# Attention kernel on one Trainium2 core: a head's second group of sums stands in one piece, a copy and the last splits are tied behind other instructions

## The chip, the cores and the metric

The kernel runs on one core of a Trainium2 chip. The metric is the time of the whole kernel on the device, in microseconds, as the median of several runs. All engines named here belong to that core: the matrix engine (PE, with PEld for its weight loads), VectorE (DVE), ScalarE (ACT), GpSimd (POOL) and SyncE (SP), whose queue issues most of the loads and stores.

## The reference

One layer of a block of 1024 tokens and 1024 channels: attention without softmax (branch A), a short gated convolution (branch B), gates, an output projection, and a feed-forward part behind it. The change lies in the attention and in the first steps of branch A:

```python
# q, k, v: (B, S, H, Dh), S = 1024, H = 16 heads, Dh = 64
for i in range(s_len // Q_BLOCK):                 # Q_BLOCK = 128
    n_keys = i * Q_BLOCK + Q_BLOCK
    z = jnp.einsum('bhqd,bhkd->bhqk', qb, kp) * inv_sqrt
    mask = s_idx < t_idx
    log_not = jnp.where(mask, jax.nn.log_sigmoid(-z), 0.0)
    excl = lax.cumsum(log_not, axis=3, reverse=True) - log_not
    a = jnp.where(mask, jnp.exp(jax.nn.log_sigmoid(z) + excl), 0.0)
    outs.append(jnp.einsum('bhqk,bhkd->bhqd', a, vp))
...
merged = (jax.nn.sigmoid(ga) * (y_a @ w_branch_a[l])
          + jax.nn.sigmoid(gb) * (y_b @ w_branch_b[l]))
```

## The kernel before

Products that need nearly full float32 precision are made from two reduced parts of each operand, a high part (`...h`, a rounded copy made by ScalarE) and a low part (`...l`, what is left, made by VectorE). So most operands exist twice, and a "split" is a ScalarE copy followed by a VectorE subtraction.

**Steps.** Attention runs over 16 heads with 8 steps each. Step i of a head treats the queries of block i against (i + 1) blocks of 128 keys. A step has four parts.

- `att_scores` makes the scores on PE (lines L922 and L923) in tiles `z` of up to 512 columns. From step 4 on there are two such tiles: the narrow one first, then one of 512 columns. There are only two buffers for `z` in PSUM (`NZ` = 2), so a third tile has to wait until the sigmoid (ScalarE, L924) has read the first. GpSimd then masks the diagonal (L927).
- `att_scan` makes running products of the sigmoids with one scan on VectorE (L937). The scan's result is multiplied on GpSimd (through the helper `tt`, L133).
- `att_trans`, for the step two before, transposes the result on PE (L952) into one of three tiles `tr`. ScalarE (L957) and VectorE (L958) copy it out as high and low part, into `afh` and `afl` for whole groups and `ath` and `atl` for the triangular rest.
- `att_av` sums attention times values on PE (L969) into the one tile `o`. A head has two groups of four query blocks; the first group takes 8 matmuls, the second 16. When a group is complete, four ScalarE instructions (L975) move it out of PSUM to `oy`, VectorE adds to it (L977), and SP stores it to `d_ya` in DRAM (L978). The next group needs `o` again, so it cannot start before these are done.

A head's second group belongs to the step 7 of that head, so its sums are made while the next head's first steps run: in the kernel before a part of them in step 2 and the last part in step 3.

**Fillers.** Between these parts PE gets "fills": three matmuls each (L1034 to L1036) of the projection of branch B, which depend on nothing in the attention. How many go where follows from a running account. Each piece of attention yields a number (`F_Z`, `F_T`, `F_S`, and `F_A` by step), and fills are written out until their sum has caught up with the attention's. The order of PE, and that of the attention's instructions on VectorE and GpSimd, is the order in the code; a scheduler places the rest. `tc.issue_after(x)` ties an instruction behind another in that scheduling.

**Values.** For each head `att_dv` makes a high part `vt` of the values on ScalarE (L863) and a low part on VectorE (L133), in steps 4 and 6 of the head before.

**Branch A's inputs.** The stored sums come back as `yr` (a load by SP, L1187, of 256 KB into a ring of four buffers) and are split into `ya` (ScalarE L1189, VectorE L133). The loop over these 16 loads stands behind the attention in the code, but with high priority, so that the first splits stand between instructions of the last two heads:

```python
yr = fq.tile([P, 512], F32, tag=("ybh", "ybl")[j % 2], bufs=2, name=nm("yr"))
nc.sync.dma_start(yr, d_ya[n][:, k, :])
h_, l_ = ya2[:, 0], ya2[:, 1]
nc.scalar.activation(h_, yr, AF.Copy)
tt(nc.vector, l_, yr, h_.bitcast(F32), ALU.subtract)
```

The first 7 loads are of the first group of queries (heads 0 to 13), and the next of the second group. In branch A itself, VectorE multiplies PE's result by a gate (L1215).

Of the kernel before, what the change touches and what calls it, by code (L numbers as in the profile page):

```python
# [9 lines left out]
F32 = mybir.dt.float32  # L10
# [11 lines left out]
H = 16  # L22
# [8 lines left out]
def block_kernel(tc, x, x_t, cols, ada_1, ada_2, ada_row, w_q, w_kv, w_cg, w_a, w_b, w_o, w_g, w_u, w_d, out):  # L31
# [799 lines left out]

    F_Z, F_T, F_S, F_A = 0.2, 0.3, 0.05, (2, 0, 0, -1.3, 0, 0, 0, -0.7)

# [20 lines left out]
    def att_dv(h, part):  # L854

        va, vb = vab["va"], vab["vb"]
        cs = slice(h % 2 * DH, h % 2 * DH + DH)
        dv = vb[:, :, cs]
        if part == 0:
            tt(nc.vector, dv, dv, va[:, :, cs], ALU.subtract)  # L860
            return
        vt = vts[h] = bp.tile([P, KT, P], F32R, tag="vt", bufs=2, name=nm("vt"))
        nc.scalar.activation(vt[:, :, :DH], dv, AF.Copy)  # L863
        tt(nc.vector, vt[:, :, DH:], dv, vt[:, :, :DH].bitcast(F32), ALU.subtract)
# [35 lines left out]
    lastav = [None]  # L900
    lastz = [None]
    lastld = [None]
    npt = [0]
# [3 lines left out]
    def att_scores(h, i):  # L907
# [11 lines left out]
        for s0 in reversed(range(0, n, 512)):  # L919
# [3 lines left out]
            lastz[0] = nc.tensor.matmul(z[:, :m], sqt[:, i * P:(i + 1) * P], skl[:, s0:s0 + m], start=False, stop=True)  # L923
            nc.scalar.activation(pt[:, off + s0:off + s0 + m], z[:, :m], AF.Sigmoid, scale=rq[:, 1, i, h:h + 1])  # L924
            if s0 + m == n:
# [7 lines left out]
    def att_scan(h, i):  # L933
        pt, off = ptof[h, i], D - (i + 1) * P
        first = pt[:, slice(D - 1, off, -2)]
        both = pt[:, slice(D - 2, off - 1 if off else None, -2)]
        nc.vector.tensor_tensor_scan(out=both, data0=first, data1=both, initial=1.0, op0=ALU.mult, op1=ALU.mult)  # L937
        mid = pt[:, slice(off + 1, D - 2, 2)]
        tt(nc.gpsimd, mid, mid, pt[:, slice(off + 2, D - 1, 2)], ALU.mult)
# [45 lines left out]
    def attention():  # L985
# [3 lines left out]
        for s in range(len(steps) + DAV):  # L989
# [24 lines left out]
            if s < len(steps):  # L1014
                yield from (a_ for q in av[:1] for a_ in itertools.islice(q, (0, 0, 0, 1, 0, 0, 1, 0)[s % 8]))
            yield from tr_
            if s < len(steps):
                att_scan(*steps[s])
            for q in av[:1]:
                yield from itertools.islice(q, 9 if s >= len(steps) else (0, 0, 2, 2, 0, 0, 2 * (s > 8 * H - 8), 2)[s % 8])  # L1020

# [162 lines left out]
    with tc.high_priority():  # L1184
        for j, (ya2, (n, k)) in enumerate(zip(ya_slots(), [(0, k) for k in range(7)] + [(1, 0), (1, 1), (1, 2), (0, 7)] + [(1, k) for k in range(3, 8)])):
# [3 lines left out]
            nc.scalar.activation(h_, yr, AF.Copy)  # L1189
            tt(nc.vector, l_, yr, h_.bitcast(F32), ALU.subtract)  # L1190
            yah[n][k], yal[n][k] = h_, l_
# [618 lines left out]
```

## Time and profile before

| what | us |
|---|---|
| three runs | 1793.41, 1792.07, 1791.86 |
| their median | 1792.07 |
| the profiled execution | 1792.89 |
| its span in the trace | 1790.9 |

The rows further down come from the profiled execution. Its span is the time from the first to the last instruction that the profiler recorded; the 2.0 us between the span and the time of that execution lie around it. Attention lies between about 596 and 957 us of the span, the end of the last head's sums and branch A between 957 and 1012. Each engine takes its instructions in order, so an instruction that waits holds up all that is queued behind it on its engine. An idle gap in front of an instruction is put down to the event that came last.

### The profile page before, as it was taken

Reading aid. Unit: us, or ns where it says so; the run is one execution under the profiler, and the core shown is the slowest. Engines: PE = TensorE matmul, PEld = TensorE weight load, DVE = VectorE, ACT = ScalarE, POOL = GpSimd, SP = SyncE. Lnnn points to the kernel's source line nnn. Section 1 sums busy time; section 2 is a strip of 40 time slices with the busy share of each in tenths; the row PEclk is TensorE's granted clock in tenths of the full one; section 3 lists DMA queues with packets and bytes.
Section 4 is the critical chain, followed back from the end, with each engine's and each line's share of the span. In section 5 each row is a group of like instructions: output and inputs, shape, how many; then the busy total and the mean of one; then the engine's idle time right before and its main releaser. Section 6 shows DMA issues by size and latency. Waiting matters only on the chain.

```text
span 1790.9 us, 24256 instructions
## 1 busy us (share of the span) xinstructions
PE 1780.1 (99%) x8355; PEld 1471.0 (82%) x8355; DVE 1268.8 (71%) x1998; ACT 826.8 (46%) x1555; POOL 345.2 (19%) x437
## 2 busy tenths in 40 slices
PE   9999999999999999999999999999999999999999
PEld 6888877888888788888888888888888888888887
DVE  6876586778774677777786674698867777644766
ACT  5534364333433567666675221764544444432320
POOL 0024333733231243333341100100000000000000
PEclk9999999999999999999999999999999999999999
DMA  9579655222634967797654866324534344399776
GB/s 384 163 249 386 234 183 165 77 95 98 231 125 149 296 199 193 196 344 186 155 139 148 305 225 201 131 94 176 201 130 151 143 188 158 134 347 324 269 232 216
DMA packets 162446, 359.03 MB, mean 200 GB/s; under 512 B 15026, under 2 KB 56330, under 8 KB 161172
## 3 DMA queue, kind: packets, MB, share of 16 engines
q1 hardware_dynamic: 125740, 289.65, 48.7%
q10 hardware_dynamic: 33096, 55.25, 8.6%
q0 software_dynamic: 3488, 12.59, 1.9%
q8 instruction: 66, 1.08, 0.3%
q14 instruction: 56, 0.46, 0.1%
HBM read 247.84 MB, written 109.62 MB: 200 GB/s over the span
## 4 chain that ended last, share of the span: by engine, by line
PE 93%; DMA 3%; DVE 1%; ACT 1%; issue 1%; POOL 0%; SPq 0%; DVEq 0%; POOLq 0%; ACTq 0%
PE e L129 8%; PE e L128 8%; PE e L127 8%; PE pj L127 7%; PE pj L129 7%; PE pj L128 7%; PE pj L294 7%; PE pj L1034 4%; PE pj L1036 4%; PE pj L1035 4%; PE e L1637 4%; PE e L1638 4%; PE e L1639 4%; PE o L969 4%; PE tr L952 3%; PE z L922 2%
## 5 line engine op out<-in xcount | busy, mean ns | idle before, releaser
L1252 ACT ACTIVATE whi<-raw 128x512 fp32r<-128x512 f32 x137 | 85.2, 630 | 162.1 <-PE e L128 101.7
L1253 DVE TENSOR_TENSOR wlo<-raw,whi 128x512 fp32r<-128x512 f32 x137 | 93.4, 689 | 69.9 <-ACT whi L1252 52.5
L128 PE MATMUL e<-big,whi 128*128 128x512 f32 x352 | 136.9, 389 | 0.0
L127 PE MATMUL e<-big,whi 128*128 128x512 f32 x352 | 136.5, 390 | 0.0
L129 PE MATMUL e<-big,wlo 128*128 128x512 f32 x352 | 136.1, 389 | 0.0
L133 POOL TENSOR_TENSOR pt<-pt 128x63 f32<-128x63 f32 (+7 forms) x128 | 95.6, 747 | 209.8 <-DVE pt L937 166.2
L294 PE MATMUL pj<-whi,big 128*128 128x512 f32 x448 | 132.5, 393 | 1.3 <-ACT big L263 1.2
L133 DVE TENSOR_TENSOR c<-pj,c 128x512 f32<-128x512 f32 x140 | 93.7, 684 | 53.6 <-PE pj L129 52.9
L924 ACT ACTIVATE pt<-z,rq 128x128 f32<-128x128 f32 (+1 forms) x192 | 106.7, 581 | 52.6 <-PE z L923 43.9
L127 PE MATMUL pj<-big,whi 128*128 128x512 f32 x320 | 124.9, 390 | 0.0
L129 PE MATMUL pj<-big,wlo 128*128 128x512 f32 x320 | 124.7, 390 | 0.0
L128 PE MATMUL pj<-big,whi 128*128 128x512 f32 x320 | 124.6, 389 | 0.0
L1638 PE MATMUL e<-wlo,f 128*128 128x512 f32 (+1 forms) x319 | 121.8, 382 | 0.0
L1637 PE MATMUL e<-whi,f 128*128 128x512 f32 (+1 forms) x319 | 121.6, 382 | 0.0
L1639 PE MATMUL e<-whi,f 128*128 128x512 f32 (+1 forms) x319 | 121.6, 382 | 0.0
L1034 PE MATMUL pj<-big,whi 128*128 128x512 f32 x256 | 113.6, 444 | 0.0
L133 DVE TENSOR_TENSOR wlo<-raw,whi 128x512 fp32r<-128x512 f32 x108 | 86.6, 805 | 33.7 <-ACT whi L524 33.7
L524 ACT ACTIVATE whi<-raw 128x512 fp32r<-128x512 f32 x108 | 67.7, 631 | 89.1 <-PE pj L128 49.8
L127 PE MATMUL e<-rh,whi 128*128 128x512 f32 x264 | 102.7, 389 | 0.0
L128 PE MATMUL e<-rl,whi 128*128 128x512 f32 x264 | 102.7, 389 | 0.0
L129 PE MATMUL e<-rh,wlo 128*128 128x512 f32 x264 | 102.0, 389 | 0.0
L1036 PE MATMUL pj<-big,wlo 128*128 128x512 f32 x256 | 100.7, 393 | 0.0
(366 smaller groups left out, 4685.6 us busy)
## 6 DMA issues: line engine op xcount, KB each, us to landing
f<-d_f SPq DMA_DIRECT2D x77, 512.0 KB, 3.6
d_f<-fs SPq DMA_DIRECT2D x70, 512.0 KB, 2.8
raw<-w_cg SPq DMA_DIRECT2D x40, 512.0 KB, 3.9
raw<-w_u SPq DMA_DIRECT2D x26, 512.0 KB, 4.9
raw<-w_g SPq DMA_DIRECT2D x25, 512.0 KB, 3.5
raw<-w_kv SPq DMA_DIRECT2D x20, 512.0 KB, 6.4
ld<-ada SPq DMA_DIRECT2D x16, 512.0 KB, 9.0
d_t<-ts SPq DMA_DIRECT2D x16, 512.0 KB, 7.0
```

The costliest lines, as they stand in the source:

```text
L127: nc.tensor.matmul(ps, wh[:, k, :], fh[:, k, :], start=(k == 0 and not onto), stop=False, skip_group_check=onto)
L128: nc.tensor.matmul(ps, wh[:, k, :], fl[:, k, :], start=False, stop=False, skip_group_check=onto)
L129: last = nc.tensor.matmul(ps, wl[:, k, :], fh[:, k, :], start=False, stop=(k == 3), skip_group_check=onto)
L133: eng.tensor_tensor(out=out, in0=a, in1=b, op=op)
L294: nc.tensor.matmul(ps, a, b, start=(k == 0 and q == 0), stop=(k == KT - 1 and q == 2))
L924: nc.scalar.activation(pt[:, off + s0:off + s0 + m], z[:, :m], AF.Sigmoid, scale=rq[:, 1, i, h:h + 1])
L1034: nc.tensor.matmul(ps, wh, rh_, start=(k == 0), stop=False)
L1036: nc.tensor.matmul(ps, wl, rh_, start=False, stop=(k == KT - 1))
L1253: los.append(nc.vector.tensor_tensor(out=lo, in0=src, in1=hi.bitcast(F32), op=ALU.subtract))
L1637: nc.tensor.matmul(o, sh, w[0][:, c], start=(j == 0), stop=False)
L1638: nc.tensor.matmul(o, sh, w[1][:, c], start=False, stop=False)
L1639: nc.tensor.matmul(o, sl, w[0][:, c], start=False, stop=(j == NJ - 1))
```

## The change

Three edits. The number and kinds of instructions of every engine stay the same, and GpSimd's order too.

1. **The second group's sums.** All 16 matmuls of a head's second group now stand in step 2 of the next head. The numbers of pieces taken in a step change (`islice`), and with `F_A` the fill that stood before step 2's transposes goes behind those of step 3. The four evacuations of the sums on ScalarE move with them.
2. **The values' copy.** `vt`'s copy on ScalarE is tied behind the sigmoid that was written last, `lastsig`.
3. **Branch A's splits.** The VectorE half of the j-th split is tied behind one scan of the list `scans`: the first behind the last scan of head 14, the next ones behind one scan of head 15 each.

```diff
--- before.py
+++ after.py
@@ -829,7 +829,7 @@
     NPT = 5
     pts = [ptp.tile([P, D], F32, name=f"pt{j}") for j in range(NPT)]
 
-    F_Z, F_T, F_S, F_A = 0.2, 0.3, 0.05, (2, 0, 0, -1.3, 0, 0, 0, -0.7)
+    F_Z, F_T, F_S, F_A = 0.2, 0.3, 0.05, (1.6, 0, -0.6, -0.3, 0, 0, 0, -0.7)
 
     def att_load(h):
         pr, e0 = h // 2, (h % 2) * DH
@@ -860,7 +860,8 @@
             tt(nc.vector, dv, dv, va[:, :, cs], ALU.subtract)
             return
         vt = vts[h] = bp.tile([P, KT, P], F32R, tag="vt", bufs=2, name=nm("vt"))
-        nc.scalar.activation(vt[:, :, :DH], dv, AF.Copy)
+        with tc.issue_after(lastsig[0].ins):
+            nc.scalar.activation(vt[:, :, :DH], dv, AF.Copy)
         tt(nc.vector, vt[:, :, DH:], dv, vt[:, :, :DH].bitcast(F32), ALU.subtract)
 
     def load_vlast(e):
@@ -899,6 +900,8 @@
     first_va = v_tile(1)
     lastav = [None]
     lastz = [None]
+    lastsig = [None]
+    scans = []
     lastld = [None]
     npt = [0]
     ats = {}
@@ -921,7 +924,7 @@
             z = pps.tile([P, 512], F32, tag="z", bufs=NZ, name=nm("z"))
             nc.tensor.matmul(z[:, :m], sqt[:, i * P:(i + 1) * P], skh[:, s0:s0 + m], start=True, stop=False)
             lastz[0] = nc.tensor.matmul(z[:, :m], sqt[:, i * P:(i + 1) * P], skl[:, s0:s0 + m], start=False, stop=True)
-            nc.scalar.activation(pt[:, off + s0:off + s0 + m], z[:, :m], AF.Sigmoid, scale=rq[:, 1, i, h:h + 1])
+            lastsig[0] = nc.scalar.activation(pt[:, off + s0:off + s0 + m], z[:, :m], AF.Sigmoid, scale=rq[:, 1, i, h:h + 1])
             if s0 + m == n:
                 diag = pt[:, D - P:]
                 nc.gpsimd.affine_select(out=diag, in_=diag, compare_op=ALU.is_ge, fill=1.0, base=-1,
@@ -934,7 +937,7 @@
         pt, off = ptof[h, i], D - (i + 1) * P
         first = pt[:, slice(D - 1, off, -2)]
         both = pt[:, slice(D - 2, off - 1 if off else None, -2)]
-        nc.vector.tensor_tensor_scan(out=both, data0=first, data1=both, initial=1.0, op0=ALU.mult, op1=ALU.mult)
+        scans.append(nc.vector.tensor_tensor_scan(out=both, data0=first, data1=both, initial=1.0, op0=ALU.mult, op1=ALU.mult))
         mid = pt[:, slice(off + 1, D - 2, 2)]
         tt(nc.gpsimd, mid, mid, pt[:, slice(off + 2, D - 1, 2)], ALU.mult)
 
@@ -1012,12 +1015,12 @@
                 av[:] = [att_av(steps[s - DAV][0], steps[s - DAV][1] // 4)]
             yield from itertools.islice(tr_, 1)
             if s < len(steps):
-                yield from (a_ for q in av[:1] for a_ in itertools.islice(q, (0, 0, 0, 1, 0, 0, 1, 0)[s % 8]))
+                yield from (a_ for q in av[:1] for a_ in itertools.islice(q, (0, 0, 1, 0, 0, 0, 1, 0)[s % 8]))
             yield from tr_
             if s < len(steps):
                 att_scan(*steps[s])
             for q in av[:1]:
-                yield from itertools.islice(q, 9 if s >= len(steps) else (0, 0, 2, 2, 0, 0, 2 * (s > 8 * H - 8), 2)[s % 8])
+                yield from itertools.islice(q, 9 if s >= len(steps) else (0, 0, 3, 0, 0, 0, 2 * (s > 8 * H - 8), 2)[s % 8])
 
     def ps_f():
         return pps.tile([P, 512], F32, tag="pj", bufs=NPJ, name=nm("pj"))
@@ -1187,7 +1190,8 @@
             nc.sync.dma_start(yr, d_ya[n][:, k, :])
             h_, l_ = ya2[:, 0], ya2[:, 1]
             nc.scalar.activation(h_, yr, AF.Copy)
-            tt(nc.vector, l_, yr, h_.bitcast(F32), ALU.subtract)
+            with tc.issue_after(scans[min(len(scans) - 9 + j, len(scans) - 1)].ins):
+                tt(nc.vector, l_, yr, h_.bitcast(F32), ALU.subtract)
             yah[n][k], yal[n][k] = h_, l_
     fqpool.close()
     gxs = ExitStack()
```

**First place: head 8, steps 2 to 4, on PE.** `o` is the tile of head 7's second group, `z_7959` the narrow scores of step 4 and `z_7966` its wide ones; `tr_7936` is step 1's transposes, made in step 3. Before:

```order
L952 MATMUL tr_7936<-dm,pt_5131 128x128 x2
L969 MATMUL o_7920<-ath_7772,vt_7419 128x512
L969 MATMUL o_7920<-atl_7773,vt_7419 128x512
L969 MATMUL o_7920<-ath_7772,vt_7419 128x384
L969 MATMUL o_7920<-atl_7773,vt_7419 128x384
L969 MATMUL o_7920<-ath_7772,vt_7419 128x256
L969 MATMUL o_7920<-atl_7773,vt_7419 128x256
L969 MATMUL o_7920<-ath_7772,vt_7419 128x128
L969 MATMUL o_7920<-atl_7773,vt_7419 128x128
L922 MATMUL z_7959<-skh_7504,sqt_7503 128x128
L923 MATMUL z_7959<-skl_7505,sqt_7503 128x128
L922 MATMUL z_7966<-skh_7504,sqt_7503 128x512
```

With the change (`z_7941` are step 3's scores, line numbers 3 higher):

```order
L972 MATMUL o_7915<-ath_7772,vt_7419 128x128
L972 MATMUL o_7915<-atl_7773,vt_7419 128x128
L925 MATMUL z_7941<-skh_7504,sqt_7503 128x512
L926 MATMUL z_7941<-skl_7505,sqt_7503 128x512
L955 MATMUL tr_7948<-dm,pt_5131 128x128 x2
L1037 MATMUL pj_7896<-big_7562,whi_7574 128x512
L1038 MATMUL pj_7896<-big_7563,whi_7574 128x512
L1039 MATMUL pj_7896<-big_7562,wlo_7575 128x512
L925 MATMUL z_7959<-skh_7504,sqt_7503 128x128
L926 MATMUL z_7959<-skl_7505,sqt_7503 128x128
L925 MATMUL z_7966<-skh_7504,sqt_7503 128x512
L926 MATMUL z_7966<-skl_7505,sqt_7503 128x512
```

The last eight sums stood behind step 3's transposes and directly in front of step 4's scores. Now all sums are over before step 3's scores, and a fill (L1037 to L1039) stands between those transposes and step 4's scores.

The same place on ScalarE, before (`ath_7627` and `afh` are evacuations of transposes, `pt_5130` the sigmoid of step 3, `pt_5131` the two of step 4):

```order
L924 ACTIVATE pt_5129<-z_7617,rq 128x384
L957 ACTIVATE ath_7627<-tr_7629 128x128
L924 ACTIVATE pt_5130<-z_7644,rq 128x512
L957 ACTIVATE ath_7627<-tr_7651 128x2x128
L975 ACTIVATE oy_7666<-o_7635,vlast 64x128 x4
L924 ACTIVATE pt_5131<-z_7674,rq 128x128
L924 ACTIVATE pt_5131<-z_7681,rq 128x512
```

With the change:

```order
L927 ACTIVATE pt_5129<-z_7617,rq 128x384
L960 ACTIVATE ath_7624<-tr_7626 128x128
L978 ACTIVATE oy_7649<-o_7630,vlast 64x128 x4
L927 ACTIVATE pt_5130<-z_7656,rq 128x512
L960 ACTIVATE ath_7624<-tr_7663 128x2x128
L927 ACTIVATE pt_5131<-z_7674,rq 128x128
L927 ACTIVATE pt_5131<-z_7681,rq 128x512
```

The four evacuations of the sums (`oy`) have moved in front of step 3's sigmoid of 512 columns and an evacuation of transposes; they stood directly in front of step 4's two sigmoids.

**Second place: the end of head 14 and the start of head 15, on VectorE.** `pt_5131` and `pt_5127` are head 14's scans of steps 6 and 7 (the view names a scan SCALAR_TENSOR_TENSOR), `ya` the splits of branch A, `wlo` and `mb` work of branch B. Before:

```order
L133 TENSOR_TENSOR ya_9906<-yr_9907,ya_9906 128x512
L958 TENSOR_TENSOR atl_9449<-tr_9450,ath_9448 128x128
L937 SCALAR_TENSOR_TENSOR pt_5131<-pt_5131 128x448
L133 TENSOR_TENSOR ya_9921<-yr_9922,ya_9921 128x512
L133 TENSOR_TENSOR ya_9911<-yr_9912,ya_9911 128x512
L133 TENSOR_TENSOR ya_9916<-yr_9917,ya_9916 128x512
L958 TENSOR_TENSOR afl_9432<-tr_9467,afh_9431 128x4x128
L958 TENSOR_TENSOR atl_9449<-tr_9477,ath_9448 128x2x128
L937 SCALAR_TENSOR_TENSOR pt_5127<-pt_5127 128x512
L1086 TENSOR_TENSOR mb_9508<-pj_9376,sgi_9374 128x512
L977 TENSOR_TENSOR oy_9491<-o_9443,oy_9491 64x512
L133 TENSOR_TENSOR wlo_9800<-raw_9793,whi_9799 128x512
```

With the change:

```order
L940 SCALAR_TENSOR_TENSOR pt_5131<-pt_5131 128x448
L961 TENSOR_TENSOR afl_9432<-tr_9467,afh_9431 128x4x128
L961 TENSOR_TENSOR atl_9449<-tr_9477,ath_9448 128x2x128
L940 SCALAR_TENSOR_TENSOR pt_5127<-pt_5127 128x512
L133 TENSOR_TENSOR ya_9901<-yr_9902,ya_9901 128x512
L1089 TENSOR_TENSOR mb_9508<-pj_9376,sgi_9374 128x512
L980 TENSOR_TENSOR oy_9491<-o_9443,oy_9491 64x512
L133 TENSOR_TENSOR wlo_9800<-raw_9793,whi_9799 128x512
L961 TENSOR_TENSOR afl_9432<-tr_9527,afh_9431 128x4x128
L961 TENSOR_TENSOR atl_9449<-tr_9537,ath_9448 128x3x128
L940 SCALAR_TENSOR_TENSOR pt_5128<-pt_5128 128x64
L133 TENSOR_TENSOR ya_9906<-yr_9907,ya_9906 128x512
```

Four of these splits stood in front of the scan of head 14's step 7. Now none does; one stands behind that scan and one behind the first scan of head 15 (`pt_5128`).

On ScalarE the copies that belong to the later splits stand in head 15 now (`ya_9921` is the fifth, `ya_9926` the sixth; `pt_5129` to `pt_5131` are the sigmoids of steps 1 to 3). With the change:

```order
L960 ACTIVATE afh_9431<-tr_9527 128x4x128
L960 ACTIVATE ath_9448<-tr_9537 128x3x128
L927 ACTIVATE pt_5129<-z_9548,rq 128x256
L1192 ACTIVATE ya_9921<-yr_9922 128x512
L960 ACTIVATE afh_9431<-tr_9555 128x4x128
L960 ACTIVATE ath_9448<-tr_9565 128x4x128
L927 ACTIVATE pt_5130<-z_9577,rq 128x384
L960 ACTIVATE ath_9584<-tr_9586 128x128
L978 ACTIVATE oy_9609<-o_9590,vlast 64x128 x4
L1192 ACTIVATE ya_9926<-yr_9927 128x512
L927 ACTIVATE pt_5131<-z_9616,rq 128x512
```

Before, `ya_9921` stood in front of the evacuation `afh_9431<-tr_9467`, among the copies ahead of head 14's last transposes; `oy` stood behind `pt_5131`, and `ya_9926` between the two sigmoids of step 4. From `pt_5129` to `oy` there were evacuations and sigmoids only.

## Rows read from the trace of the kernel before

**Rows 1.** The page: busy time, share of the span and instructions of each engine.

```profile
PE 1780.1 (99%) x8355; PEld 1471.0 (82%) x8355; DVE 1268.8 (71%) x1998; ACT 826.8 (46%) x1555; POOL 345.2 (19%) x437
```

**Rows 2.** PE's weight loads' waits, 590 to 1015: waiter <- awaited: us, times, longest.

```profile
PEld z L922 <- ACT pt L924: 3.9, 16, 0.3
```

**Rows 3.** Timeline, PE, head 8: start, duration, line, tiles, count, [idle before, releaser].

```profile
783.86 0.38 PE L952 MATMUL tr<-dm,pt 128*128 128x128 f32 x2
784.00 0.47 PE L969 MATMUL o<-ath,vt 128*128 128x512 f32 x1
...
785.19 0.27 PE L969 MATMUL o<-atl,vt 128*128 128x128 f32 x1
785.30 0.28 PE L922 MATMUL z<-skh,sqt 128*128 128x128 f32 x1
...
785.53 0.44 PE L922 MATMUL z<-skh,sqt 128*128 128x512 f32 x1
785.81 0.40 PE L923 MATMUL z<-skl,sqt 128*128 128x512 f32 x1
786.05 0.49 PE L952 MATMUL tr<-dm,pt 128*128 128x128 f32 x3
786.29 0.49 PE L1034 MATMUL pj<-big,whi 128*128 128x512 f32 x1
...
787.08 0.28 PE L922 MATMUL z<-skh,sqt 128*128 128x256 f32 x1
787.20 0.28 PE L923 MATMUL z<-skl,sqt 128*128 128x256 f32 x1
787.51 0.50 PE L922 MATMUL z<-skh,sqt 128*128 128x512 f32 x1
787.85 0.39 PE L923 MATMUL z<-skl,sqt 128*128 128x512 f32 x1
```

**Rows 4.** Timeline of ScalarE, the same head.

```profile
784.12 0.69 ACT L924 ACTIVATE pt<-z,rq 128x512 f32<-128x512 f32 x1 [2.02 <-PE z L923]
...
785.50 1.13 ACT L975 ACTIVATE oy<-o,vlast 64x128 f32<-64x128 f32 x4 [0.41 <-PE o L969]
786.52 0.93 ACT L924 ACTIVATE pt<-z,rq 128x128 f32<-128x128 f32 x2
```

**Rows 5.** Timeline of PE, head 14, step 5.

```profile
926.55 0.45 PE L922 MATMUL z<-skh,sqt 128*128 128x512 f32 x1
```

**Rows 6.** Timeline of PE, the transposes of head 14's step 6.

```profile
937.24 0.28 PE L923 MATMUL z<-skl,sqt 128*128 128x256 f32 x1
938.67 0.66 PE L952 MATMUL tr<-dm,pt 128*128 128x128 f32 x4 [1.16 <-POOL pt L133]
```

**Rows 7.** Timeline of VectorE, ahead of head 14's last scan.

```profile
932.67 2.70 DVE L133 TENSOR_TENSOR ya<-yr,ya 128x512 fp32r<-128x512 f32 x3
...
936.22 1.21 DVE L937 TENSOR_TENSOR_SCAN pt<-pt 128x512 f32<-128x512 f32 x1
```

**Rows 8.** Timeline of ScalarE and of SP's queue, head 15 and behind.

```profile
937.61 0.47 ACT L924 ACTIVATE pt<-z,rq 128x256 f32<-128x256 f32 x1 [0.51 <-PE z L923]
...
959.67 1.27 SPq L1187 DMA_DIRECT2D yr<-d_ya  x3
...
962.63 0.63 ACT L1189 ACTIVATE atl<-yr 128x512 fp32r<-128x512 f32 x1 [1.58 <-DMA yr<-d_ya]
```

**Rows 9.** Groups by line: busy, mean ns of one, idle before and its releaser.

```profile
L958 DVE TENSOR_TENSOR afl<-tr,afh 128x512 fp32r<-128x512 f32 x64 | 44.0, 687 | 15.4 <-ACT afh L957 14.8
...
L957 ACT ACTIVATE afh<-tr 128x512 fp32r<-128x512 f32 x64 | 38.4, 600 | 17.7 <-PE tr L952 17.7
```

**Rows 10.** Timeline of PE, branch A's start.

```profile
1008.39 0.47 PE L1034 MATMUL pj<-ya,whi 128*128 128x512 f32 x1 [0.28 <-DVE sgi L1215]
```

**Rows 11.** Timeline of GpSimd: two multiplications of 447 columns, heads 7 and 14.

```profile
773.19 0.93 POOL L133 TENSOR_TENSOR pt<-pt 128x447 f32<-128x447 f32 x1 [1.79 <-DVE pt L937]
...
932.90 1.23 POOL L133 TENSOR_TENSOR pt<-pt 128x447 f32<-128x447 f32 x1 [2.40 <-ACT ya L1189]
```

## The prediction

> **What bounds the kernel now.** The page's busy line comes first: the matrix engine (PE) is busy for 99% of the span [rows 1], so nothing on the other engines counts unless it makes PE wait, and no work is added or taken away here. What can change is the sum of PE's waits in the attention stage (596 to 957 us) and in branch A behind it. The view of waits names them: PE's weight loads for scores waited 16 times for a sigmoid, 3.9 us in all [rows 2]. The timeline of one head shows where. In head 8 the scores of step 5 are ready to go at 787.32 (787.20 and a 128x256 matmul's 0.12, the distance of 787.08 and 787.20) and start at 787.51; the next start is 0.34 later instead of 0.23 [rows 3]. So a head loses 0.19 + 0.11 = 0.30 us there. The reason stands on ScalarE: the scores have two PSUM tiles (`NZ`), the third to come needs the sigmoid of step 4's second tile, and this one comes after four evacuations of sums, which begin at 785.50, 0.31 after the last matmul of the sums (785.19); ScalarE then goes to the next activation at 786.52 [rows 4]. Heads 1 to 13 have this wait. In head 14 a fill stands between the two scores of step 5 and there is none (no idle time in the row) [rows 5].
>
> **A head's second group summed in one piece.** PE keeps its instructions, but the eight last matmuls of the sums now come before step 3's scores, and a fill comes after step 3's transposes. On ScalarE the four evacuations move in front of step 3's sigmoid. Step 4's second scores need the PSUM tile that this sigmoid reads. I lay both engines out from the last matmul of the sums as zero, with head 8's durations.
>
> PE [rows 3]: 0.11 to step 3's scores (785.19 to 785.30); 0.28 for their first matmul behind a narrow one (785.53 to 785.81); 0.24 for the second (785.81 to 786.05); 0.14 for two transposes (783.86 to 784.00); 0.79 for the fill (786.29 to 787.08); 0.23 for step 4's two narrow scores (785.30 to 785.53). PE is ready for step 4's second scores at 1.79.
>
> ScalarE [rows 4]: evacuations begin at 0.31, step 3's sigmoid 1.02 later (785.50 to 786.52) and lasts 0.69 (the row at 784.12); PE goes on 0.06 after a sigmoid's end (786.52 + 0.93 = 787.45, against 787.51 [rows 3]). That is 2.08.
>
> So PE waits 0.29 at a new place; behind a wait the following start is 0.34 instead of 0.28 away (+0.06), and one more pair of wide scores stands behind a narrow matmul (0.28 for 0.23, +0.05). New cost 0.40, old cost 0.30: +0.10 a head. Step 5's wait should go, since step 4's sigmoid no longer queues behind the evacuations: it waits only for its own scores and is done about 0.3 us before PE asks. Heads 1 to 13: 13 x 0.10 = +1.3 us. Head 14 had no wait to give back: +0.40, of which some 0.05 were there, so +0.35. Bounds for a head: -0.30 (no new wait at all) and +0.40 (the old one stays too).
>
> **Values' copy behind the sigmoid.** One ScalarE instruction changes places with the first-needed sigmoid of step 5, a head's only move there. PE asks for that tile again at step 6's second scores, behind four transposes, a fill and the first scores; the old order did not make it wait there. Zero either way; if that cover went, one copy's 0.5 us a head would show.
>
> **Branch A's splits behind scans.** Before, three splits (2.70 us, each also waiting for its ScalarE half) stand ahead of head 14's last scan on VectorE [rows 7], and PE's transposes of that step start at 938.67, 1.31 after the 937.36 at which PE was free (937.24 and 0.12) [rows 6]. The tie puts the splits behind the scan. 2.70 is more than 1.31, so I take the whole 1.31 as won.
>
> What is late next is the ring of four loads `yr`. The fifth load needs the first split, which now stands behind this scan, and ScalarE's copy of the fifth stands in the order right behind the sigmoid of head 15's step 1 and in front of an evacuation that the sums need. The scan ended at 937.43 (936.22 + 1.21) [rows 7]; it moves up by at least 1.31 and at most 2.70, so its end is 934.7 to 936.1. Add a split, 0.69, and the load: issued 959.67, first reader at 962.63, so 2.96 [rows 8]. It is there at 938.4 to 939.8; ScalarE comes free at 938.08 (937.61 + 0.47) [rows 8], waits 0.3 to 1.7 and copies for 0.52 (a copy is 0.63 long and overlaps its neighbour by 0.1): the evacuation is 0.8 to 2.2 late. From the transposes' start PE has two sets of four transposes (some 0.34 each, since three take 0.24, 786.05 to 786.29 [rows 3]), two fills (0.79), one set of scores and a first sum (about 0.7) before the matmul that needs it: 3.0 us, against the 0.72 that ScalarE needs to come free there, then 0.60 and 0.69 of evacuation [rows 9], so some 0.95 is free. Loss 0 to 1.3; I take 0.8, nearer the late end, because the order in front of the scan keeps two evacuations. The sixth copy stands between head 15's four evacuations and its step 3 sigmoid: 0.40 + 0.52 = 0.9. Last head: -1.31 + 0.8 + 0.9 = +0.4; bounds -0.9 and +1.3 with a load of this length.
>
> The load's price can also be had from the Trainium skill, "DMA: Bandwidth & Descriptors", section "Anatomy of one DMA": about 2.0 us fixed and the bytes at 436 GB/s, which makes an estimated 2.6 us for 256 KB. By it the copy would wait 0.36 less and the last head come out near zero; the trace's 2.96 decides.
>
> **Branch A's own order.** The wait of PE at 1008.39, 0.28 for VectorE's product [rows 10], can go (the sums end earlier in PE's order, and what hangs on them too) or grow (VectorE has one more 1.2 us reduction in front of that product). I take -0.3, with bounds -0.5 and +0.5.
>
> Sum: +1.3 + 0.35 + 0.4 - 0.3 = +1.75, say +1.8. The profiled execution took 1792.89 us (its span 1790.9 and 2.0 around it), so it would be 1794.7; it stands 0.8 above the median of the runs shown. From the median 1792.07: **1793.9 us**, +0.1%. That is less than the 0.2%, 3.6 us, that a measurement of this kernel can tell from no change.
>
> **Rivals.**
> 1. *Faster: no new wait at step 4.* If step 3's sigmoid ends before PE is ready, 0.29 sooner than I have it, the 0.30 of 13 heads (3.9), the 1.31 and the 0.5 of branch A all go: -5.7, 1786.4. For it: it takes 0.29 only, and the first evacuation reads just the columns that are final earliest. Against it: in the trace that first evacuation starts only behind the last matmul [rows 3, 4], and the order of both queues is fixed. 0.13.
> 2. *Slower: ScalarE stands still behind late loads.* The copies wait in the middle of head 15, and each split frees the next load. If a load takes 3 us longer than the one in the row, it comes on top where no slack is left, first at the fifth copy and then, by half, at the sixth: +1.8 + 3 + 1.5 = +6.3, 1798.4. It decides from 0.5 us over the row on. For it: the ring has four buffers and the queue issues in order. Against it: few other transfers run there. 0.17.
> 3. *The tied splits meet the multiplication.* A scan's end releases GpSimd's multiplication, and the split now starts at that moment. The trace shows such a multiplication of 447 columns at 1.23 us beside splits and at 0.93 without [rows 11]. With 0.30 more on six multiplications in head 15, of which I let all gate PE, this gives +1.8 + 1.8 = +3.6, 1795.7; slack of about 1 us at most of them speaks against it. 0.12. The Trainium skill, "SBUF — State Buffer", section "Who interferes with whom", has such a rule: a VectorE instruction with two SBUF inputs and a GpSimd one that reads SBUF lock each other out for a whole instruction. By it the price would be a whole split each time; the trace shows less than half of one.
> 4. *The trade comes out even*, the new waits as long as those removed: 1791 to 1793. 0.18.
>
> **How the numbers follow.** My forecast (+1 to +3) has 0.40. Slower by over 0.2% comes from rival 2 and a part of rival 3: 0.20. Faster by over 0.2% is nearly all of rival 1: 0.13. The rest, 0.67, is within it. The range leaves out most of rival 1 and the upper part of rival 2: 1788.5 to 1797.0.
>
> **What will show it.** In the changed profile: scores of step 4 (not 5) with an idle gap near 0.3 and an activation as releaser, in heads 1 to 14; ScalarE's four evacuations directly before a 128x512 sigmoid; no wait of over 1 us at head 14's last transposes; a ScalarE wait for `yr` in head 15, with sums late behind it. I am wrong if the scores' waits vanish altogether, if step 5's wait stays beside the new one (+5), or if PE's waits of head 15 exceed 3 us.

## The result and the profile after

| | median us | runs |
|---|---|---|
| before | 1792.52 | 15 |
| changed | 1795.36 | 15 |

The ratio is 1.0016 (95% interval 1.0008 to 1.0023): +2.8 us, slower by less than the 0.2% taken as the bound. The changed kernel's profiled execution took 1797.45 us, the longest of its 15, so its span (1795.7) is not set against the old one; what is compared is PE's time head by head. The page's busy line and three of the waits of PE's weight loads (590 to 1020 us) answer to [rows 1, 2]:

```profile
PE 1781.3 (99%) x8355; PEld 1471.4 (82%) x8355; DVE 1269.3 (71%) x1998; ACT 825.0 (46%) x1555; POOL 341.9 (19%) x437
```

```profile
PEld z L925 <- ACT pt L927: 6.6, 16, 0.8
PEld tr L955 <- POOL pt L133: 5.9, 9, 1.6
PEld tr L955 <- DVE afl L961: 1.3, 3, 0.7
```

Busy times are the same within 0.1% on PE and DVE. Scores still wait 16 times for a sigmoid, but 6.6 us instead of 3.9. The place has moved, as PE's timeline of head 8 shows (answers to [rows 3]):

```profile
788.08 0.27 PE L972 MATMUL o<-atl,vt 128*128 128x128 f32 x1
788.19 0.44 PE L925 MATMUL z<-skh,sqt 128*128 128x512 f32 x1
...
788.84 0.47 PE L1037 MATMUL pj<-big,whi 128*128 128x512 f32 x1
...
789.67 0.27 PE L926 MATMUL z<-skl,sqt 128*128 128x128 f32 x1
790.14 0.50 PE L925 MATMUL z<-skh,sqt 128*128 128x512 f32 x1 [0.19 <-ACT pt L927]
790.47 0.39 PE L926 MATMUL z<-skl,sqt 128*128 128x512 f32 x1
```

And ScalarE's, same head (answers to [rows 4]):

```profile
788.39 1.12 ACT L978 ACTIVATE oy<-o,vlast 64x128 f32<-64x128 f32 x4 [2.35 <-PE o L972]
789.40 0.68 ACT L927 ACTIVATE pt<-z,rq 128x512 f32<-128x512 f32 x1
```

The last sums stand at 788.08, the evacuations begin 0.31 later, step 3's sigmoid starts 1.01 behind them and ends at 790.08, and PE goes on 0.06 after that. It was ready at 789.79 (789.67 and 0.12).

**PE's lost time by head.** For all that follows, the starts of neighbouring matmuls were taken from the trace, and from each distance the usual one for that width (0.23 us for 512 columns, 0.12 for 256); excesses over 0.045 us are summed from a head's first scores to the next head's. Some 0.42 us a head are left where nothing waits.

```
us lost by PE            0+1    2     3     6     8     12    14    15    branch A
before                   3.44  0.74  0.74  0.89  0.72  0.74  0.48  2.06  0.70
changed                  4.91  1.46  0.83  1.59  0.83  0.81  0.82  2.36  0.91
sums only                3.32  1.46  0.82  1.60  0.83  0.83  0.84  3.14  0.45
copy only                4.32  0.73  0.73  0.88  0.72  0.73  0.42  2.13  0.43
splits only              3.46  0.73  0.73  0.88  0.72  0.73  0.49  0.99  0.69
late evacuation          4.02  1.37  1.37  1.54  1.38  0.69  1.77  3.01  1.42
sums, add late           3.59  2.18  1.20  2.08  1.32  1.18  1.33  3.14  0.53
change, late evacuation  3.73  2.12  1.51  2.38  1.83  1.55  1.10  2.35  0.74
late evacuation, add     3.83  0.65  1.11  0.81  0.76  0.47  1.05  2.48  1.10
all three                3.18  0.67  1.14  0.85  0.79  0.42  0.48  1.32  2.05
splits and fill          3.36  0.42  0.42  0.59  0.42  0.42  0.42  0.92  0.49
behind transposes        3.72  0.42  0.47  0.58  0.42  0.42  0.42  0.59  0.48
change, fills shifted    3.43  0.83  0.83  0.99  1.57  0.94  0.84  2.27  1.36
change, behind transp.   2.56  1.15  0.42  1.11  1.01  0.42  0.85  1.45  0.79
```

Heads 3, 8 and 12 stand for those between; in the runs with late evacuations these differ among themselves. In heads 0 and 1 the engines also wait for transfers of branch B: ScalarE 1.6 us for weights before and 1.9 changed, VectorE 1.0 and 1.9 for the load of a `cy`. These heads differ by 0.9 us between the kernel before and the copy-only one, so the 1.5 us between two single executions there is put to no edit, though head 1 has the new wait at step 4 too. Branch A differs by up to 0.3 in the same way.

### The profile page after: what moved, and what is told of

The parts are those of the page before. It is cut to its first block, busy times and chain, and to the rows that moved or that the text cites. A ratio compares the mean times of both kernels' runs of the same rounds, so it can differ in the third digit from the quotient of the medians.

```text
span 1795.7 us, 24256 instructions
## 1 busy us (share of the span) xinstructions
PE 1781.3 (99%) x8355; PEld 1471.4 (82%) x8355; DVE 1269.3 (71%) x1998; ACT 825.0 (46%) x1555; POOL 341.9 (19%) x437
## 4 chain that ended last, share of the span: by engine, by line
PE 91%; DMA 3%; ACT 2%; DVE 2%; issue 1%; POOL 1%; SPq 0%; POOLq 0%; ACTq 0%; DVEq 0%
PE e L128 8%; PE e L129 8%; PE e L127 8%; PE pj L127 7%; PE pj L129 7%; PE pj L128 7%; PE pj L294 7%; PE e L1641 4%; PE e L1642 4%; PE e L1643 4%; PE pj L1037 4%; PE pj L1039 4%; PE pj L1038 4%; PE o L972 4%; PE tr L955 3%; PE e L1378 2%
## 5 line engine op out<-in xcount | busy, mean ns | idle before, releaser
L133 POOL TENSOR_TENSOR pt<-pt 128x63 f32<-128x63 f32 (+7 forms) x128 | 100.2, 783 | 200.5 <-DVE pt L940 165.5
L129 PE MATMUL pj<-big,wlo 128*128 128x512 f32 x320 | 124.7, 390 | 0.0
L1037 PE MATMUL pj<-big,whi 128*128 128x512 f32 x256 | 114.6, 448 | 0.0
L940 DVE TENSOR_TENSOR_SCAN pt<-pt 128x64 f32<-128x64 f32 (+7 forms) x128 | 96.1, 750 | 10.2 <-POOL pt L930 9.1
```

Source lines behind the costliest of these rows:

```text
L129: last = nc.tensor.matmul(ps, wl[:, k, :], fh[:, k, :], start=False, stop=(k == 3), skip_group_check=onto)
L133: eng.tensor_tensor(out=out, in0=a, in1=b, op=op)
L940: scans.append(nc.vector.tensor_tensor_scan(out=both, data0=first, data1=both, initial=1.0, op0=ALU.mult, op1=ALU.mult))
L1037: nc.tensor.matmul(ps, wh, rh_, start=(k == 0), stop=False)
```

## The experiments

Each is compared with the kernel before on the same chip.

**Sums only.** The change without its two ties:

```diff
-        with tc.issue_after(lastsig[0].ins):
-            nc.scalar.activation(vt[:, :, :DH], dv, AF.Copy)
+        nc.scalar.activation(vt[:, :, :DH], dv, AF.Copy)
...
-            with tc.issue_after(scans[min(len(scans) - 9 + j, len(scans) - 1)].ins):
-                tt(nc.vector, l_, yr, h_.bitcast(F32), ALU.subtract)
+            tt(nc.vector, l_, yr, h_.bitcast(F32), ALU.subtract)
```

> Only the sums are moved (the change's first edit); the values' copy and branch A's splits stand as before. Theory: the move alone carries the loss. In the heads without a delay on GpSimd the wait moves from step 5 to step 4 (idle gap 0.19 instead of 0.03 to 0.05, and +0.085 us a head, as in the trace of the changed kernel); in heads 1, 2 and 6, where a fill's VectorE work stands between the evacuation and step 3's scan, step 3's product comes late on GpSimd and costs some 0.5 more each; head 14's last transposes keep their 1.3 us. Sum: +1.1, +0.35 and +1.5, so 1.5 to 3.5 us slower than before. Rival (the splits carry the loss): within 1.5 us of before.

Measured: 1796.49 against 1792.95, ratio 1.0020 (1.0011 to 1.0029): +3.5 us. The steady heads lose 0.09 more each, heads 2 and 6 some 0.7 each, head 14 0.36; head 1 does not. Head 15, whose cost the expectation left out, loses 1.1: 0.9 of it in front of step 4's scores (950.35), where a copy `ya` stands between the four evacuations and step 3's sigmoid, as in the changed kernel. So this edit alone loses at least as much as the whole change.

**Copy only.** To the kernel before:

```diff
+        with tc.issue_after(lastsig[0].ins):
+            nc.scalar.activation(vt[:, :, :DH], dv, AF.Copy)
```

> Only the values' copy is tied behind the sigmoid of step 5. Theory: no cost and no gain, within 0.5 us of before by the starts of scores head by head (heads 3 to 13 each within 0.03 us of before). Rival (VectorE's low part of the values, which stands behind the copy, holds up the scan of step 5 or 6): 0.1 to 0.5 us a head, 1.5 to 7 us slower, with transposes that wait for GpSimd.

Measured: 1792.94 against 1792.95, 0.9998 (0.9989 to 1.0007). Heads 2 to 13 are within 0.03 of before each. The tie costs and brings nothing.

**Splits only.** To the kernel before:

```diff
+            with tc.issue_after(scans[min(len(scans) - 9 + j, len(scans) - 1)].ins):
+                tt(nc.vector, l_, yr, h_.bitcast(F32), ALU.subtract)
```

> Only branch A's splits are tied behind the scans. Theory: the 1.3 us of head 14's last transposes go; in head 15 ScalarE waits for the fifth load and some 0.8 us come back there; the sixth copy stands between step 4's two sigmoids, as before, so the 1.0 us wait of the changed kernel at step 4 isn't there. Net -0.3 us (-0.8 to +0.2) over heads 14 and 15, the other heads unchanged. Rival (the late loads cost more than the stall that they remove): +0.5 to +1.5 over heads 14 and 15.

Measured: 1790.92 against 1792.95, 0.9990 (0.9981 to 0.9999): faster by 2.0 us, of which the trace shows 1.07 in head 15. The 0.8 that I expected to come back did not, though ScalarE waits for the fifth load just as long (first fence; in the changed kernel 1.17). PE's timeline (second fence) has two fills (six matmuls) between the transposes whose evacuation stands behind that copy and the next ones, where the changed kernel has one:

```profile
939.76 0.64 ACT L1191 ACTIVATE ya<-yr 128x512 fp32r<-128x512 f32 x1 [1.20 <-DMA d_mb<-mb]
```

```profile
937.83 0.60 PE L954 MATMUL tr<-dm,pt 128*128 128x128 f32 x4
938.18 0.48 PE L1036 MATMUL pj<-big,whi 128*128 128x512 f32 x1
...
938.96 0.40 PE L1036 MATMUL pj<-big,whi 128*128 128x512 f32 x1
...
939.65 0.60 PE L954 MATMUL tr<-dm,pt 128*128 128x128 f32 x4
```

**Late evacuation.** To the kernel before; the four evacuations go behind step 4's sigmoids:

```diff
+        if g:
+            yield 0
         yv = bp.tile([DH, 512], F32, tag="oy", bufs=2, name=nm("oy"))
...
+            with tc.issue_after(lastsig[0].ins) if g and h < H - 1 else ExitStack():
-... islice(q, (0, 0, 0, 1, 0, 0, 1, 0)[s % 8])
+... islice(q, (0, 0, 0, 1, 1, 0, 1, 0)[s % 8])
-... islice(q, ... (0, 0, 2, 2, 0, 0, 2 * (s > 8 * H - 8), 2)[s % 8])
+... islice(q, ... (0, 0, 2, 1, 0, 0, 2 * (s > 8 * H - 8), 2)[s % 8])
```

> The kernel before, but the four evacuations of a head's second group are tied behind step 4's two sigmoids (heads 0 to 14); PE's order stays. Theory: step 5's wait is there only because step 4's sigmoids queue behind the evacuations, so it goes: -0.30 us a head in heads 1 to 13, -3.9 us (-3 to -4.5), and nothing new. Rival (ScalarE is short anyway and the wait comes up at step 6, or the transposes' evacuations come late for the next sums): between -1 and +2 us, with a new gap at step 6 or in front of the first group's sums.

Measured: 1801.41 against 1792.95, 1.0045 (1.0033 to 1.0058). Both theories missed: the scores' wait went but for 1.3 us in all, and transposes now wait for GpSimd's product, 0.73 in head 7, less in heads 9 to 13. Head 7, ScalarE, VectorE and PE:

```profile
768.58 1.11 ACT L979 ACTIVATE oy<-o,vlast 64x128 f32<-64x128 f32 x4
769.58 0.48 ACT L958 ACTIVATE ath<-tr 128x384 fp32r<-128x384 f32 x1
```

```profile
770.09 0.56 DVE L959 TENSOR_TENSOR atl<-tr,ath 128x384 fp32r<-128x384 f32 x1 [1.68 <-ACT ath L958]
770.68 0.69 DVE L981 TENSOR_TENSOR oy<-o,oy 64x512 f32<-64x512 f32 x1
771.30 0.81 DVE L938 TENSOR_TENSOR_SCAN pt<-pt 128x320 f32<-128x320 f32 x1
```

```profile
773.03 0.66 PE L953 MATMUL tr<-dm,pt 128*128 128x128 f32 x4 [0.73 <-POOL pt L133]
```

Two things hold up step 4's scan: the low part `atl`, which waits for the evacuation `ath` behind the four others, and the addition.

**Sums, with the addition late.** To the sums-only kernel, with step 3 taking one piece more:

```diff
+        if g:
+            yield 0
         nc.vector.tensor_tensor(out=yv, in0=o[DH:], in1=yv, op=ALU.add)
```

> As the run with the sums alone moved, but VectorE's addition of the evacuated sums (and its store) stands behind step 3's scan instead of in front of it. Theory: in heads 2 and 6 the scan came late because that addition waited for the evacuations at the head of VectorE's queue, with a fill's product behind it; so the 0.69 us of each of these heads go (each then 0.05 to 0.15), the 0.19 us gap at step 4's second scores stays in all heads: 1.2 to 1.6 us faster than the sums-only run, 1.7 to 2.3 us slower than before. Rival (the late sigmoid of step 3 alone makes the scan late, or the fill's product): heads 2 and 6 keep at least 0.5 us each.

Measured: 1800.97 against 1793.43, 1.0041 (1.0029 to 1.0054). The theory fell: heads 2 and 6 got worse (2.18 and 2.08), others too. Behind the scan the addition pushes the values' subtraction `vb` into GpSimd's product, where it takes 1.10 instead of 0.67, and the next scans come later.

**The change with late evacuation.** Sums in step 2, evacuations (tie as above) and addition in step 3, behind its scan:

```diff
+            with tc.issue_after(lastsig[0].ins) if g and h < H - 1 else ExitStack():
-... (0, 0, 3, 0, 0, 0, 2 * (s > 8 * H - 8), 2)[s % 8])
+... (0, 0, 3, 1, 0, 0, 2 * (s > 8 * H - 8), 2)[s % 8])
```

> The changed kernel, but the four evacuations of a second group (heads 0 to 14) are tied behind step 3's sigmoid, and VectorE's addition stands behind step 3's scan. Theory: step 4's wait was the queueing of that sigmoid behind the evacuations, so no scores wait in heads 3 to 13: 0.46 us a head less than the changed kernel at that place, and step 5's wait does not come back, since step 4's sigmoids have the fill in front of their scores. 5 to 7.5 us faster than the changed kernel, 2.5 to 4.5 faster than before. Rival (ScalarE is short, the wait comes up elsewhere): the gap moves to step 5, as in the kernel before, and the gain over the changed kernel is 1 to 2.5 us.

Measured: 1805.19 against 1793.43, 1.0065 (1.0053 to 1.0078). Both missed: most of the waits of PE's weight loads are now transposes that wait for GpSimd (18.8 us in all, 590 to 1025 us), and scores still wait for a sigmoid 26 times, 7.1 us.

**Late evacuation with the addition behind the scan.** As the late evacuation, with the last piece taken after step 4's scan:

```diff
-... (0, 0, 2, 2, 0, 0, 2 * (s > 8 * H - 8), 2)[s % 8])
+... (0, 0, 2, 1, 1, 0, 2 * (s > 8 * H - 8), 2)[s % 8])
```

> The kernel before with the evacuations tied behind step 4's sigmoids, as in the run that lost 8 us, but with VectorE's addition behind step 4's scan. Theory: that run lost because the addition stood in front of the scan and waited there for the late evacuations, so that GpSimd's product and the transposes came late by 0.73 us a head; the addition's place alone turns it round: no wait for GpSimd in heads 3 to 13, no wait for a sigmoid either, 3 to 4.5 us faster than before. Rival (the late evacuations hold up the transposes' evacuations on ScalarE): still 2 us or more slower than before, with the same gap at the transposes.

Measured: 1794.98 against 1793.43, 1.0007 (0.9998 to 1.0017), between the two ranges. The addition's place explains much of the 8 us but not all; head 3 still loses 1.11.

**All three.** The same, with the copy and the splits tied as in the change.

> The kernel before, with the copy tied behind the sigmoid and the splits tied behind scans as in the change, and with the evacuations behind step 4's sigmoids and the addition behind step 4's scan; the sums stay in steps 2 and 3. Theory: the gains add, 3.9 us of the scores' waits and 1.2 us of the splits: 4.5 to 6 us faster than before. Rival (the sixth copy, which now stands ahead of step 4's sigmoids in head 15, waits for its load there): 1 us of it is lost in head 15, with a scores' gap of about 0.7 us at its step 4 or 5.

Measured: 1793.08 against 1793.43, 0.9995 (0.9986 to 1.0005). Both missed. The splits' gain is there (head 15: 1.32); the scores' gain is not in heads 3 to 8. Branch A lost 1.4 more in this execution, in waits for ScalarE's weight copies (0.71 at 960.32) and for VectorE's product with the gate (0.47 and 0.44 at 1008.88 and 1014.89).

**Splits and fill.** The splits-only kernel, with one fill moved between step 5's two scores:

```diff
             if s0:
-                yield F_Z
+                yield F_Z + (0.8 if i == 5 and h else 0)
-        yield F_Z + F_S * ((i - 1) % 8 + 1) + (F_A[i] if h else 0)
+        yield F_Z + F_S * ((i - 1) % 8 + 1) + (F_A[i] if h else 0) - (0.8 if i == 5 and h else 0)
```

> The kernel before with the splits tied behind the scans (as in the splits-only run), and with the fill that stands just behind step 5's scores (behind its transposes in heads 1 and 2) put between the narrow and the wide scores, as heads 14 and 15 have it already; ScalarE's order stays. Theory: step 5's wait goes because 0.7 us of other work now covers it, and nothing hangs on that fill. PE's lost time a head falls from 0.74 to 0.42 us in heads 1 to 13, which is 4.0 us, and the splits give 1.2: 4.5 to 6 us faster than before. Rival (step 5's later wide scores hand the wait on to its scan, to GpSimd and to the transposes of step 7, as in the runs with late evacuations): at least 0.25 us a head comes back there, 1 to 2.5 us faster than before.

Measured: 1788.10 against 1792.89, 0.9977 (0.9969 to 0.9986): 4.8 us faster than before, as the theory had it, while the changed kernel was 2.8 slower. Nothing waits in step 5 of head 8:

```profile
786.25 0.28 PE L925 MATMUL z<-skl,sqt 128*128 128x256 f32 x1
786.37 0.40 PE L1036 MATMUL pj<-big,whi 128*128 128x512 f32 x1
...
787.06 0.39 PE L924 MATMUL z<-skh,sqt 128*128 128x512 f32 x1
787.28 0.39 PE L925 MATMUL z<-skl,sqt 128*128 128x512 f32 x1
```

**Evacuation behind the transposes' own.** All three, with another tie:

```diff
-            with tc.issue_after(lastsig[0].ins) if g and h < H - 1 else ExitStack():
+            with tc.issue_after(lastth[0].ins) if g and h < H - 1 else ExitStack():
```

(`lastth` is ScalarE's last evacuation of transposes, L961 there.)

> As the run with all three, but the late evacuations are tied behind ScalarE's evacuation of step 4's transposes, so this one comes before them. Theory: the runs with late evacuations lost their gain because that evacuation of transposes stood behind four others, VectorE's low part waited for it at the head of its queue, and the scan of step 4 behind it came late; so the small waits for GpSimd at step 6 go too, and PE's lost time falls to 0.42 us in heads 3 to 13: 0.23 less in heads 4 to 8, 0.7 and 0.45 less in heads 3 and 11. 1.5 to 4 us faster than the run with all three. Rival (ScalarE has no place for four evacuations in steps 4 and 5 at all): heads 3 to 8 keep 0.65 us or more and step 5's scan is late in the place of step 4's.

Measured: 1788.28 against 1792.89, 0.9973 (0.9963 to 0.9983). Heads 2 to 14 stand at 0.42 to 0.47 but for head 6 (0.58), and the gain over the run with all three is above the 4 us expected, since branch A and head 15 are lower here as well. So the place of `ath` was the other half of what the late evacuations had lost.

**The change with its fills shifted.**

```diff
-    HEAD, TAIL = 16, 10.0
+    HEAD, TAIL = 15, 10.0
```

> The changed kernel with one fill fewer ahead of the attention (15 for 16), which shifts the fills against the heads. In the changed kernel VectorE's product and split of a finished branch B block stand around step 3's scan in heads 2 and 6 alone, and these two lose 1.46 and 1.59 us of PE's time where other heads lose 0.83. Here neither head has that product ahead of step 3's scan nor the split behind it. Theory: the extra 0.65 to 0.75 us belongs to these VectorE instructions, so heads 2 and 6 fall to 0.75 to 1.1 us. Rival (it belongs to what else happens in heads 2 and 6, such as their loads): both stay above 1.3 us. The heads from 7 on get another pattern of fills and are not compared.

Measured: 1797.43 against 1792.89, 1.0026 (1.0016 to 1.0037). Heads 2 and 6 lose 0.83 and 0.99: the extra belonged to the fills' VectorE work. The whole is slower because of the heads from 7 on (head 8: 1.57).

**The change with evacuations behind the transposes' own.** The same tie and piece on the changed kernel:

```diff
-... (0, 0, 3, 0, 0, 0, 2 * (s > 8 * H - 8), 2)[s % 8])
+... (0, 0, 3, 0, 1, 0, 2 * (s > 8 * H - 8), 2)[s % 8])
```

> The changed kernel (second group's sums all in step 2, copy and splits tied) with the evacuations of heads 0 to 14 tied behind ScalarE's evacuation of step 4's transposes and VectorE's addition behind step 4's scan, as in the run before this one. Theory: the place of the sums on PE costs nothing by itself; the change lost through where the evacuations and the addition came to stand. So heads 2 to 14 fall to 0.42 us each (from 0.83, and from 1.46 and 1.59 in heads 2 and 6); in head 15 the wait behind the fifth copy stays (0.4 to 0.8 us more there than in the run that has the sums in two pieces). 5.5 to 7.5 us faster than the changed kernel, 3 to 5 faster than before. Rival (one piece of 16 sums costs by itself): heads 3 to 13 keep at least 0.6 us each, at most 4 us faster than the changed kernel.

Measured: 1791.33 against 1793.11, 0.9991 (0.9982 to 1.0000), short of the 3 us expected. Heads 3 and 12 fall to 0.42, so 16 sums in one piece cost nothing there. Heads 2 and 6 keep 1.1: a fill's product `cy` still stands directly ahead of step 3's scan in them, which the sums' place decides through the fills. In head 2 it starts at 648.12, the scan at 648.72, and the transposes that wait for GpSimd at 650.51 lose 0.66; in head 6 they lose 0.46. The extra of head 8 (1.01) is spread over several places, the largest of them 0.24 in front of step 4's wide scores.

## Why the prediction was right, point by point

The forecast was 1793.9, from a sum of +1.8; measured is +2.8, in the range and on the side forecast. One term failed, that of heads 2 and 6; the fifth load's came out near its number partly by luck; branch A's is within what two executions differ by.

- *The new wait at step 4.* Forecast 0.29 and a new cost of 0.40 a head, for 0.30 given back. The trace has 0.35 (790.14 less 789.79) and lost times of 0.83 and 0.74 over the 0.42 that is always there: 0.41 new, 0.32 old. Step 5's wait went. Head 14: +0.35 forecast, +0.34 measured.
- *Heads 2 and 6: the step that failed.* I wrote "heads 1 to 13: 13 x 0.10", so one head stood for all, and I followed the sums only along PE and ScalarE to the scores. On VectorE the addition moved too: before, it stood behind step 3's scan, now it stands ahead of it. And with the sums the fills moved: in heads 2 and 6 a fill's product (`cy`) now stands between the addition and that scan, and its split (`ybl`) behind. Head 2 before, then with the change on VectorE, GpSimd and PE:

```profile
648.40 0.68 DVE L937 TENSOR_TENSOR_SCAN pt<-pt 128x256 f32<-128x256 f32 x1
649.60 0.69 DVE L977 TENSOR_TENSOR oy<-o,oy 64x512 f32<-64x512 f32 x1 [0.52 <-ACT oy L975]
```

```profile
650.74 0.69 DVE L980 TENSOR_TENSOR oy<-o,oy 64x512 f32<-64x512 f32 x1 [2.39 <-ACT oy L978]
651.46 0.69 DVE L1057 TENSOR_TENSOR cy<-pj,cy 128x512 f32<-128x512 f32 x1
652.07 0.41 DVE L961 TENSOR_TENSOR atl<-tr,ath 128x256 fp32r<-128x256 f32 x1
652.40 0.68 DVE L940 TENSOR_TENSOR_SCAN pt<-pt 128x256 f32<-128x256 f32 x1
653.00 0.67 DVE L133 TENSOR_TENSOR vb<-vb,va 128x512 f32<-128x512 f32 x1
653.59 1.10 DVE L1061 TENSOR_TENSOR ybl<-cy,ybh 128x512 fp32r<-128x512 f32 x1
```

```profile
653.17 0.97 POOL L133 TENSOR_TENSOR pt<-pt 128x255 f32<-128x255 f32 x1 [1.53 <-DVE pt L940]
654.09 0.74 POOL L930 TENSOR_SCALAR_AFFINE_SELECT pt<-pt 128x128 f32<-128x128 f32 x1
```

```profile
653.40 0.39 PE L926 MATMUL z<-skl,sqt 128*128 128x512 f32 x1
654.19 0.66 PE L955 MATMUL tr<-dm,pt 128*128 128x128 f32 x4 [0.40 <-POOL pt L133]
```

  The addition waits until the evacuations are over, then `cy` takes its 0.69, and the scan starts 1.66 after the addition. In head 8, without a `cy`, it starts 1.19 after it:

```profile
789.54 0.69 DVE L980 TENSOR_TENSOR oy<-o,oy 64x512 f32<-64x512 f32 x1 [2.20 <-ACT oy L978]
790.38 0.42 DVE L961 TENSOR_TENSOR atl<-tr,ath 128x256 fp32r<-128x256 f32 x1
790.73 0.68 DVE L940 TENSOR_TENSOR_SCAN pt<-pt 128x256 f32<-128x256 f32 x1
```

  GpSimd's product takes 0.97 beside `vb` in both heads; in head 2 it ends at 654.14, and PE's transposes wait for it. The two heads cost +0.72 and +0.70 where 0.10 each was in the sum: +1.2 us. The run with shifted fills has the addition ahead of the scan but no `cy`, and the extra is gone. The last run above (the change with evacuations behind the transposes' own) has `cy` there but not the addition, and these transposes still wait. So it is the fill's product; the addition ahead of the scan does not make them wait by itself. The split `ybl` comes behind that scan and is not in the way of these transposes.
- *Head 14's last transposes.* The 1.31 went: no gap at 942.38 (below; answers to [rows 6]).
- *The fifth load.* Forecast 0.8. PE loses 0.43 and 0.34 at the two places below (0.26 and 0.18 idle), but only the second hangs on the load. From issue (row of SP's queue below) to the first reader at 944.28 the load took 2.97, as in [rows 8]. (The store `d_mb` that the row names was issued behind the load and landed later, at 944.87; the load had landed at 944.21.) ScalarE waits 1.17 there, the low part that the sum at 946.18 needs comes at 945.44, and the sum is late. The transposes at 943.95 wait for an earlier low part, at 943.20. ScalarE's half of it stands at 940.63, ahead of the load's copy; the low part is late because it stands on VectorE behind the first tied split and three more instructions (VectorE's rows below). The forecast has nothing there, so it is luck that the two together make 0.8. In the splits-only run these VectorE instructions stand in the same order, and a second fill in front of those transposes covers it, which the moved sums' fill numbers took away. The estimate of 2.6 in the prediction would have been too short. The Trainium skill, "DMA: Bandwidth & Descriptors", section "Anatomy of one DMA", gives its fit for transfers that GpSimd issues, and SP issued this one.
- *The sixth copy.* Forecast 0.9; step 4's scores wait 0.69 idle (below), some 0.9 more than their usual distance; the sums-only run shows the same wait. Sum of the last head: +0.4 forecast, +0.30 measured.

```profile
942.26 0.28 PE L926 MATMUL z<-skl,sqt 128*128 128x256 f32 x1
942.38 0.60 PE L955 MATMUL tr<-dm,pt 128*128 128x128 f32 x4
...
943.95 0.66 PE L955 MATMUL tr<-dm,pt 128*128 128x128 f32 x4 [0.26 <-DVE afl L961]
...
946.18 0.50 PE L972 MATMUL o<-afl,vt 128*128 128x512 f32 x1 [0.18 <-DVE afl L961]
...
951.58 0.53 PE L925 MATMUL z<-skh,sqt 128*128 128x512 f32 x1 [0.69 <-ACT pt L927]
```

  The rows of ScalarE (answer to [rows 8]), VectorE and SP's queue that go with it:

```profile
940.63 0.60 ACT L960 ACTIVATE afh<-tr 128x512 fp32r<-128x512 f32 x1
...
944.28 0.63 ACT L1192 ACTIVATE ya<-yr 128x512 fp32r<-128x512 f32 x1 [1.17 <-DMA d_mb<-mb]
...
949.31 1.12 ACT L978 ACTIVATE oy<-o,vlast 64x128 f32<-64x128 f32 x4 [2.79 <-PE o L972]
950.32 0.63 ACT L1192 ACTIVATE ya<-yr 128x512 fp32r<-128x512 f32 x1
950.84 0.68 ACT L927 ACTIVATE pt<-z,rq 128x512 f32<-128x512 f32 x1
```

```profile
940.58 0.67 DVE L133 TENSOR_TENSOR ya<-yr,ya 128x512 fp32r<-128x512 f32 x1
941.16 0.69 DVE L1089 TENSOR_TENSOR mb<-pj,sgi 128x512 f32<-128x512 f32 x1
941.88 0.69 DVE L980 TENSOR_TENSOR oy<-o,oy 64x512 f32<-64x512 f32 x1
942.49 0.68 DVE L133 TENSOR_TENSOR wlo<-raw,whi 128x512 fp32r<-128x512 f32 x1
943.20 0.69 DVE L961 TENSOR_TENSOR afl<-tr,afh 128x512 fp32r<-128x512 f32 x1
...
945.44 0.69 DVE L961 TENSOR_TENSOR afl<-tr,afh 128x512 fp32r<-128x512 f32 x1 [0.30 <-ACT afh L960]
```

```profile
941.31 0.32 SPq L1190 DMA_DIRECT2D yr<-d_ya  x1
```

- *Branch A.* Forecast -0.3, measured +0.2 in one execution; kernels with the old order of sums and evacuations lie between 0.43 and 0.70 there, and the sums-only run at 0.45, so its sign stays open.
- *The copy.* Forecast zero, and zero by its own run.
- *Rivals.* The first (no new wait) fell with the 0.35. The second (late loads) was there in kind but no worse than forecast. The third was right about the size and not about the price: the tied splits of head 15 do meet GpSimd's multiplications (128x63 takes 0.65 at 944.64, where it takes 0.29 at 621.74 in head 1; four wider ones take 0.29 to 0.36 more), but none of PE's waits in that head stands behind one. The even trade is the copy's case only.

Heads 2 to 15 and branch A add up to +3.2 in the two traces, against the +2.8 of the medians; with heads 0 and 1 it is +4.7, of the 4.8 us between the two spans.

## What to carry to other kernels

Follow a moved instruction through every queue in which something waits for it, not only to the consumer that the change is about: here the moved evacuations reached PE by the sigmoid, which was priced to 0.01 us, and the moved sums shifted the fills, whose product on VectorE came to stand ahead of a scan, which was not priced. Look for heads in which other work stands at the same place; one head taken for all hides them. And where a wait is short, moving independent work of the waiting engine into it (a fill between two scores: 0.74 to 0.42 us a head) was simpler than moving what it waits for (six attempts, from +12 to -5 us).

## What the runs showed of the hardware

A VectorE instruction with both inputs in SBUF and a GpSimd one hold each other up in turn: `ybl` took 1.10 beside the product that ends at 654.14, and the mask select right behind it 0.74, where the one at 651.35, beside `cy`, takes 0.29. `cy`, with one input in PSUM, kept its 0.69. The Trainium skill, "SBUF — State Buffer", section "Who interferes with whom", states this as a lock for a whole instruction between VectorE with two SBUF inputs and GpSimd's reads; the trace agrees (of the 1.10, 0.55 lie before the product's end and 0.55 behind it). In the prediction I had read less than half a split from [rows 11]. The rows here fit a price of what is left of the other instruction, not of a whole one: `vb` still had 0.50 to run when the product started, and the product took 0.97 where one of that width takes 0.61 (649.17 in the kernel before).
